# The opening of a hybrid decoder block: normalised on tokens and turned once, raw first products scaled in their banks

## The chip, the cores and the metric

The kernel runs on one core of a Trainium2 chip. A core has a matrix engine (TensorE, PE in the profile, with its weight loads as PEld), a vector engine (VectorE, DVE), a scalar engine (ScalarE, ACT), GpSimd (POOL) and SyncE (SP), which here only issues DMA transfers. Each engine works through its own queue in order and waits there for semaphores that others raise. The metric is the device time of one execution in microseconds; lower is better. Times of single instructions come from one profiled execution.

## The reference

One decoder layer for 256 tokens of width 2048 in float32: a half-step SwiGLU feed-forward, a mixer, a second half-step feed-forward and a last norm. Only the beginning of the first feed-forward matters here:

```python
def rms_norm(x, gain):
    var = jnp.mean(xf * xf, axis=-1, keepdims=True)
    return (xf * lax.rsqrt(var + NORM_EPS) * gain).astype(x.dtype)

def swiglu_ffn(x, w_gate, w_up, w_down):
    return (jax.nn.silu(x @ w_gate) * (x @ w_up)) @ w_down

x = x + 0.5 * swiglu_ffn(rms_norm(x, ffn1_norm), w_gate, w_up, w_down)
```

The norm's factor, rsqrt(var + eps), is one number for each token, and the gain is one number for each of the 2048 columns. `w_gate` and `w_up` are 2048 x 5632. So a product of tokens that are not yet scaled can be put right afterwards, row by row, while sums of products taken with Strassen's scheme need tokens that are scaled already.

## The kernel before, in words

**Layout.** `xres` holds x with tokens on the 128 partitions, in two halves (t = 0, 1), loaded in four pieces of 512 columns (`load_x(c)`, 0.5 MB each). TensorE needs x turned: columns on partitions. A column unit u (0 to 3) is 512 columns of x, four blocks j of 128. A turned unit is kept as a rounded high part and a remainder, low part. A weight block (`raw_g` of the gate matrix, `raw_u` of the up matrix) is 512 x 512, 1 MB; `load` issues its DMA from SP and `parts_of` splits it: ACT rounds it to the high part (`hi`, a CAST), DVE subtracts to get the low part (`lo`, a TENSOR_TENSOR). A product of a block with both token halves is 24 matmuls (`multiply`): 16 with `hi` and 8 with `lo`.

**The first 512 hidden columns** (the opening) are computed in the usual way from eight blocks, in the order g0, u0, g1, u1, g2, u2, g3, u3 (letter for the matrix, number for the column unit), into four PSUM banks, `ps_g` and `ps_u` for each token half. After that the hidden columns are computed 1024 at a time by Strassen's scheme for the units 0 and 1 and usually for the units 2 and 3 (`seven`): products named a, c, e, d, with block differences on DVE (`raw_g<-raw_g,raw_g`). The first of these, product a, then c, then e, follow the opening on TensorE. They need tokens that are scaled by the norm's factor, and three sums of them (`seven_of`, tiles `xs`).

**How the opening before makes its tokens.** `norm.turn` transposes unit u of the raw x on TensorE (`pt_n`), ACT takes it times the gain as the high part (`xT_n`), DVE takes the remainder. All eight blocks are multiplied by these raw units, and the factor comes in at the end, with the Silu and the last multiply (`sg<-ps_g,r_n`, `sg<-ps_u,r_n`). For the products that follow, the units are made a second time: `norm.factor` works the factor out from the sums of squares (`norm.squares`), `norm.rows` spreads it over the partitions (`diag_n`, `pb_n`, `bc_n`), `plain` puts high and low together again (units 0 and 1 on DVE, units 2 and 3 by ACT straight from the transpose's bank), and `normalise` multiplies by the spread factor on DVE (`v<-v,bc_n`), rounds on ACT (CAST `x<-v`) and subtracts on DVE (`x<-v,x`).

**What sets the order.** `Engine.pinned` (line 35) is a switch: while it is on, the instructions of PE, ACT and DVE stay in the order in which the program writes them; while it is off, a scheduler orders them. It is on until block u1 has been multiplied (line 532) and off from there. A loaded block takes one of three buffers (`raws`) and its load waits until DVE has made the low part of the block three before; SP issues loads in order, so a waiting load holds back those behind it. The first two blocks of `seven` go to two other buffers (`kept`). Splits have three buffers in rotation in all.

## Time and profile before

| | us |
|---|---|
| median of 3 runs (lowest to highest) | 1749.13 (1748.94 to 1749.91) |
| the profiled execution: its time | 1750.54 |
| the profiled execution: its span, first to last instruction | 1748.6 |
| TensorE busy | 1724.4 |
| VectorE busy | 1491.9 |
| ScalarE busy | 1045.3 |

The profiled execution is 1.41 us above the median of the runs; 1.94 us of its time lie around the span. A row of the timeline gives the start, the time from the first start to the last end of a merged group, the engine, the line (L42 is the wrapper through which PE, ACT and DVE instructions are recorded, so tiles tell more than lines), the operation, out<-in, and in brackets what ended idle time before it.

### The profile page before, as it was taken

How to read it: one execution, taken by the hardware profiler on the slowest of the kernel's cores; microseconds unless marked ns; L12 is line 12 of the kernel's file. 1: busy time of each engine (PE TensorE's matmuls, PEld its weight loads, DVE VectorE, ACT ScalarE, POOL GpSimd, SP SyncE). 2: the span in 40 equal slices, each digit the busy share in tenths (PEclk: the TensorE clock that was granted, in tenths of full speed). 3: DMA queues.
4: the chain of work that ended last, by engine and by line, in shares of the span. 5: the costliest groups of instructions: out<-in, count | busy, mean ns of one | idle time of the engine just before them, and what ended most of it. 6: DMA issues, size and time to landing. Idle time of an engine off the chain costs nothing. (4 is left out here: it accounts for less than half of the span.)

```text
span 1748.6 us, 20335 instructions
## 1 busy us (share of the span) xinstructions
PE 1724.4 (99%) x8031; PEld 1436.9 (82%) x8031; DVE 1491.9 (85%) x1247; ACT 1045.3 (60%) x1354; POOL 6.9 (0%) x32
## 2 busy tenths in 40 slices
PE   8899999999999999999999999999999999999997
PEld 6688788888888888888888888888788888888876
DVE  7988989889789888587987668989799887899885
ACT  6665565666465666574755455666566664656654
POOL 1000000000000000000000000000000000000000
PEclk9999999999999999999999999999999999999999
DMA  7465655674565665556555664574475546555743
GB/s 280 148 205 187 217 192 194 216 258 155 185 203 189 211 219 180 184 166 197 180 195 184 233 198 139 195 263 167 170 245 200 209 144 237 192 193 193 256 169 105
DMA packets 173904, 343.24 MB, mean 196 GB/s; under 512 B 5620, under 2 KB 8048, under 8 KB 173680
## 3 DMA queue, kind: packets, MB, share of 16 engines
q1 hardware_dynamic: 173344, 340.82, 56.9%
q8 instruction: 63, 1.03, 0.2%
q10 hardware_dynamic: 144, 1.05, 0.2%
q14 instruction: 33, 0.27, 0.0%
q0 software_dynamic: 320, 0.07, 0.0%
HBM read 339.82 MB, written 2.10 MB: 196 GB/s over the span
## 5 line engine op out<-in xcount | busy, mean ns | idle before, releaser
L42 ACT CAST hi_g_p<-raw_g 128x1024 fp32r<-128x1024 f32 x140 | 142.5, 1048 | 103.8 <-DVE raw_g L42 29.8
L42 DVE TENSOR_TENSOR lo_g_p<-raw_g,hi_g_p 128x2048 fp32r<-128x2048 f32 x70 | 159.6, 2288 | 31.9 <-ACT hi_g_p L42 31.8
L42 ACT CAST hi_u_p<-raw_u 128x1024 fp32r<-128x1024 f32 x140 | 140.8, 1048 | 74.0 <-PE ps_u_a L42 26.6
L42 DVE TENSOR_TENSOR lo_u_p<-raw_u,hi_u_p 128x2048 fp32r<-128x2048 f32 x70 | 159.1, 2286 | 19.5 <-ACT hi_u_p L42 19.2
L42 PE MATMUL ps_d<-hi_d,h 128*128 128x512 f32 x704 | 167.9, 390 | 0.0
L42 PEld LDWEIGHTS ps_d<-hi_d,h 128*128 128x128 f32 x704 | 131.5, 188 | 26.8
L42 PE MATMUL ps_in<-xT_nm,hi_in 128*128 128x512 f32 x640 | 153.3, 391 | 0.0
L42 PEld LDWEIGHTS ps_in<-xT_nm,hi_in 128*128 128x128 f32 x640 | 117.4, 188 | 23.2 <-ACT tha L42 0.4
L42 ACT CAST hi_d<-raw_d 128x1024 fp32r<-128x1024 f32 x88 | 88.2, 1047 | 68.0 <-PE ps_u_d L42 22.4
L42 DVE TENSOR_TENSOR lo_d<-raw_d,hi_d 128x2048 fp32r<-128x2048 f32 x44 | 100.6, 2290 | 31.4 <-ACT hi_d L42 31.4
L42 DVE TENSOR_TENSOR lo_in<-raw_in,hi_in 128x2048 fp32r<-128x2048 f32 x40 | 91.4, 2286 | 39.1 <-ACT hi_in L42 36.9
L42 ACT CAST hi_in<-raw_in 128x1024 fp32r<-128x1024 f32 x80 | 80.1, 1046 | 67.2 <-PE ps_in L42 45.7
L42 ACT CAST hi_d_p<-raw_d 128x1024 fp32r<-128x1024 f32 x84 | 84.3, 1046 | 50.8 <-DVE raw_d L42 39.6
L42 ACT CAST hi_g_x<-raw_g 128x1024 fp32r<-128x1024 f32 x80 | 81.5, 1048 | 45.5 <-PE ps_g_c L42 26.8
L42 DVE TENSOR_TENSOR lo_d_p<-raw_d,hi_d_p 128x2048 fp32r<-128x2048 f32 x42 | 95.4, 2288 | 11.7 <-ACT hi_d_p L42 11.6
L42 ACT CAST hi_u_x<-raw_u 128x1024 fp32r<-128x1024 f32 x80 | 80.5, 1047 | 33.3 <-PE ps_u_c L42 20.7
L42 DVE TENSOR_TENSOR raw_u<-raw_u,raw_u 128x2048 f32<-128x2048 f32 x40 | 91.6, 2290 | 8.7 <-DMA raw_u<-in_ffn_w_up_dram 8.0
L42 DVE TENSOR_TENSOR raw_g<-raw_g,raw_g 128x2048 f32<-128x2048 f32 x40 | 91.5, 2289 | 7.7 <-DMA raw_g<-in_ffn_w_gate_dram 7.3
L42 DVE TENSOR_TENSOR lo_g_x<-raw_g,hi_g_x 128x2048 fp32r<-128x2048 f32 x40 | 91.5, 2288 | 4.0 <-ACT hi_g_x L42 3.9
L42 DVE TENSOR_TENSOR lo_u_x<-raw_u,hi_u_x 128x2048 fp32r<-128x2048 f32 x40 | 91.4, 2285 | 0.8 <-ACT hi_u_x L42 0.6
L42 PE MATMUL ps_d<-lo_d,h 128*128 128x512 f32 x352 | 87.3, 389 | 0.0
L42 PEld LDWEIGHTS ps_in<-xT_nm,lo_in 128*128 128x128 f32 x640 | 82.1, 191 | 3.1
(346 smaller groups left out, 3583.6 us busy)
## 6 DMA issues: line engine op xcount, KB each, us to landing
raw_u<-in_ffn_w_up_dram SPq DMA_DIRECT2D x88, 1024.0 KB, 5.1
raw_d<-in_ffn_w_down_dram SPq DMA_DIRECT2D x88, 1024.0 KB, 5.1
raw_g<-in_ffn_w_gate_dram SPq DMA_DIRECT2D x87, 1024.0 KB, 5.1
raw_in<-in_w_in_dram SPq DMA_DIRECT2D x40, 1024.0 KB, 5.0
raw_o<-in_w_out_dram SPq DMA_DIRECT2D x16, 1024.0 KB, 5.1
xres<-in_x_dram SPq DMA_DIRECT2D x4, 512.0 KB, 8.5
fin<-in_final_norm_dram ACTq DMA_DIRECT2D x1, 1024.0 KB, 6.8
out_dram<-xres SPq DMA_DIRECT2D x4, 256.0 KB, 2.7
```

Source lines behind the costliest of these rows:

```text
L42: ins = getattr(self.engine, name)(*args, **kwargs)
```

## The change

The opening is written out as a function of its own, `begin`, in a fixed order from its first instruction to its last.

- Only unit 0 is still turned raw. Its two blocks, g0 and u0, are multiplied with the raw unit, and then their four banks are multiplied in place by the factor (`scaled`, a DVE TENSOR_SCALAR from PSUM to PSUM). The remaining blocks accumulate on top.
- The other units, and unit 0 a second time, are scaled on tokens by ACT (`tokens`: a copy of 128 x 512 with the factor as its scale), then transposed (`turned_tokens`), and split with the gain straight into the tiles `x` that the later products use (`high` on ACT, `low` on DVE). `rows` and `normalise` are no longer used in the opening; `plain` is used for the units 0 and 1 alone.
- x is loaded ahead: the pieces 1 and 2 right behind block g0, whose last piece now goes ahead of x; block u0 comes in two halves with piece 3 of x between them.
- Squares are shared between DVE and ACT (five and three; six and two before), and the factor is worked out before the second half of u0 is split.
- The first block of `seven` is loaded and split inside `begin` and handed over (`ready`). The Silu and the last multiply of the opening take no factor any more.

The second feed-forward keeps its way (`begin_after`). The diff, cut to its core:

```diff
+            def begin():
+                Engine.pinned = True
...
+                raw = {("g", 0): first_columns("g", 0, pieces=pieces)}
+                load_x(1)
+                load_x(2)
+                raw["u", 0] = first_columns(
+                    "u", 0, pieces=((0, 2), (2, 4)), loaded=lambda i: load_x(3) if i == 0 else None
+                )
+                for m, u in (("g", 1), ("u", 1)):
+                    raw[m, u] = first_columns(m, u)
...
+                norm.squares(0, (dve, dve))
+                for c in (1, 2):
+                    norm.squares(c, (dve, act))
+
+                def tokens(u):
+                    n = [keep(f"n{tag}_{u}_{t}") for t in range(NT)]
+                    for t in range(NT):
+                        act.activation(n[t], xres[:, t, u * CW : (u + 1) * CW], AF.Copy, scale=norm.r[:, t : t + 1])
+                    return n
+
+                def turned_tokens(u, n):
+                    pts = []
+                    for j in range(UK):
+                        pt = bank(f"pt{tag}_{u}_{j}")[:, :S]
+                        for t in range(NT):
+                            pe.transpose(pt[:, t * P : (t + 1) * P], n[t][:, j * P : (j + 1) * P], ident)
+                        pts.append(pt)
+                    return pts
+
+                def high(u, pts):
+                    for j, pt in enumerate(pts):
+                        act.activation(units[u][:, j, :S], pt, AF.Copy, scale=gain[:, UK * u + j : UK * u + j + 1])
+
+                def low(u, pts):
...
+                        dve.scalar_tensor_tensor(lo, pt, g, f32(hi), op0=ALU.mult, op1=ALU.subtract)
...
+                def scaled(banks):
+                    for t in range(NT):
+                        dve.tensor_scalar(banks[t], banks[t], norm.r[:, t : t + 1], None, op0=ALU.mult)
+
+                def work_out(i):
+                    if i == 2:
+                        norm.squares(3, (dve, act))
+                        norm.factor()
...
+                blk = parts("u", 0, between=work_out)
+                multiply(targets(ups, 0, norm.xT[0]), blk, js=(0, 1))
+                n, pts = tokens(1), []
+                multiply(
+                    targets(ups, 0, norm.xT[0]), blk, js=(2, 3), middle=lambda: pts.extend(turned_tokens(1, n))
+                )
+                scaled(gps)
...
+                def between_parts(i):
+                    if i == 2:
+                        high(1, pts)
+                        low(1, pts)
+
+                blk = parts("g", 1, between=between_parts)
+                raw["g", 2] = first_columns("g", 2)
+                n0 = tokens(0)
+                scaled(ups)
+                multiply(targets(gps, 1, units[1]), blk, True)
+                pts0 = turned_tokens(0, n0)
+                blk = parts("u", 1)
+                raw["u", 2] = first_columns("u", 2)
+                high(0, pts0)
+                low(0, pts0)
+                n2, pts2 = tokens(2), []
+                multiply(targets(ups, 1, units[1]), blk, True, middle=lambda: pts2.extend(turned_tokens(2, n2)))
+                plain(1, units[1])
+                plain(0, units[0])
+                blk = parts("g", 2)
+                raw["g", 3] = first_columns("g", 3)
+                high(2, pts2)
+                low(2, pts2)
+                n3, pts3 = tokens(3), []
+                multiply(targets(gps, 2, units[2]), blk, True)
+                sums()
+                blk = parts("u", 2)
+                raw["u", 3] = first_columns("u", 3)
+                sums()
+                multiply(targets(ups, 2, units[2]), blk, True, middle=lambda: pts3.extend(turned_tokens(3, n3)))
+                blk = parts("g", 3)
+                high(3, pts3)
+                low(3, pts3)
+                multiply(targets(gps, 3, units[3]), blk, True)
+                blk = parts("u", 3)
+                w11 = load(wg[: UK * P, CW : 2 * CW], f"g{tag}_first", kept=True)
+                ready.append((w11, parts_of(w11, f"g{tag}_first", split=lambda i: None)))
+                multiply(targets(ups, 3, units[3]), blk, True)
+                Engine.pinned = False
+                for t in range(NT):
+                    sg = keep(f"sg{tag}_0_{t}")
+                    act.activation(sg, gps[t], AF.Silu)
+                    dve.tensor_tensor(sg, ups[t], sg, op=ALU.mult)
...
-                follow = {
-                    (1, "g"): [norm.rows, lambda: plain(0)],
-                    (1, "u"): [flush, lambda: normalise(0), lambda: plain(1)],
-                    (2, "g"): [lambda: normalise(1), sums],
-                    (2, "u"): [lambda: normalise(2), sums],
-                    (3, "g"): [lambda: normalise(3)],
-                }
```

In three places the rows of the engines' queues show what moves. The names are tiles, with numbers that tell buffers apart.

On SP, from its second row, before: x and the blocks of unit 0.

```order
L93 DMA xres<-in_x_dram 128x2x512
L165 DMA raw_g_0_0_119<-in_ffn_w_gate_dram 128x512 x2
L93 DMA xres<-in_x_dram 128x2x512
L165 DMA raw_g_0_0_119<-in_ffn_w_gate_dram 128x2x512
L165 DMA raw_u_0_0_177<-in_ffn_w_up_dram 128x4x512
```

The same place after the change.

```order
L93 DMA xres<-in_x_dram 128x2x512
L165 DMA raw_g_0_0_119<-in_ffn_w_gate_dram 128x512 x2
L165 DMA raw_g_0_0_119<-in_ffn_w_gate_dram 128x2x512
L93 DMA xres<-in_x_dram 128x2x512 x2
L165 DMA raw_u_0_0_125<-in_ffn_w_up_dram 128x2x512
```

The rest of g0 goes ahead of x, pieces 1 and 2 of x go ahead of u0, and u0 comes in halves; piece 3 of x and the second half follow.

On DVE, before, from the low parts of the turned unit 2 to the low parts of block g2: the units 0 and 1 are being scaled (`v<-v,bc_n`), put together (`v<-xT_n`) and split again (`x<-v,x`).

```order
L42 SCALAR_TENSOR_TENSOR xT_n_2_319<-pt_n_11_338,cols_first,xT_n_2_319 128x256
L42 TENSOR_TENSOR v_0_0_302<-v_0_0_302,bc_n_300 128x512
L42 TENSOR_TENSOR v_0_1_303<-v_0_1_303,bc_n_300 128x512
L42 TENSOR_TENSOR v_1_0_376<-xT_n_1_194 128x512
L42 TENSOR_TENSOR x_0_369<-v_0_0_302,x_0_369 128x4x128
L42 TENSOR_TENSOR x_0_369<-v_0_1_303,x_0_369 128x4x128
L42 TENSOR_TENSOR v_1_1_377<-xT_n_1_194 128x512
L42 TENSOR_TENSOR lo_g_0_2_383<-raw_g_0_2_380,hi_g_0_2_382 128x1024 x2
```

On DVE, after, from the second scaled bank pair to the low parts of block g2.

```order
L42 TENSOR_SCALAR ps_u_0_1_118<-ps_u_0_1_118,r_n_216 128x512
L42 TENSOR_TENSOR lo_u_0_1_326<-raw_u_0_1_131,hi_u_0_1_325 128x1024 x2
L42 SCALAR_TENSOR_TENSOR x_0_198<-pt_0_0_313,cols_first,x_0_198 128x256
L42 SCALAR_TENSOR_TENSOR x_0_198<-pt_0_1_316,cols_first,x_0_198 128x256
L42 SCALAR_TENSOR_TENSOR x_0_198<-pt_0_2_319,cols_first,x_0_198 128x256
L42 SCALAR_TENSOR_TENSOR x_0_198<-pt_0_3_322,cols_first,x_0_198 128x256
L42 TENSOR_TENSOR v_1_0_381<-x_1_199 128x512
L42 TENSOR_TENSOR v_1_1_382<-x_1_199 128x512
L42 TENSOR_TENSOR v_0_0_385<-x_0_198 128x512
L42 TENSOR_TENSOR v_0_1_386<-x_0_198 128x512
L42 TENSOR_TENSOR lo_g_0_2_390<-raw_g_0_2_281,hi_g_0_2_389 128x1024 x2
```

The multiplications by the spread factor and the second split of each unit are gone; the low part of a unit is taken once, from the bank of the scaled transpose, and the banks are scaled in place.

On ACT, before, the high parts of block g3 stand ahead of the roundings of unit 1 and of the sums `xs`.

```order
L42 ACTIVATE v_3_1_389<-pt_n_15_412,cols_first 128x128
L42 CAST hi_g_0_3_506<-raw_g_0_3_504 128x1024 x2
L42 CAST x_1_443<-v_1_0_376 128x4x128
L42 CAST x_1_443<-v_1_1_377 128x4x128
L42 CAST hi_u_0_3_545<-raw_u_0_3_543 128x1024 x2
L42 CAST xs_0_450<-spare_452 128x4x128
```

On ACT, after, around the blocks u2 and g3.

```order
L42 CAST xs_0_433<-spare_435 128x4x128
L42 CAST hi_u_0_2_439<-raw_u_0_2_331 128x1024 x2
L42 CAST xs_0_433<-v_0_0_385 128x4x128
L42 CAST xs_1_434<-v_0_1_386 128x4x128
L42 CAST xs_1_434<-v_1_0_381 128x4x128
L42 CAST hi_g_0_3_492<-raw_g_0_3_395 128x1024 x2
L42 ACTIVATE x_3_201<-pt_3_0_472,cols_first 128x256
```

The roundings of the sums `xs`, whose inputs DVE makes, now stand ahead of the high parts of block g3, and these ahead of the high parts of unit 3.

More of the change, by code (lines that the diff above doesn't have):

```diff
@@ L212, in __init__, with squares @@
             self.ss = work.tile([P, NT, NC_D], F32, tag="ss", name=f"ss_{name}")
-        def squares(self, c, engine=None):
-            for t in range(NT):
+        def squares(self, c, engines=(act, act)):
+            for t, engine in enumerate(engines):
                 x, part = xres[:, t, c * CW : (c + 1) * CW], self.ss[:, t, c : c + 1]
@@ L345, in quad, with seven @@
         return tile.rearrange("p (j c) -> p j c", j=UK)
-    def seven(w, rows, cols, sf, xs, name, keep, done, between=None):
+    def seven(w, rows, cols, sf, xs, name, keep, done, between=None, ready=None):
         a, c, e, d = (bank(f"ps_{name}_{n}") for n in "aced")
@@ new lines, in begin_after @@
+                units.append(big(f"x{tag}_3"))
+                for t in range(NT):
+                    sg = keep(f"sg{tag}_0_{t}")
+                    act.activation(sg, ps["g", t], AF.Silu, scale=norm.r[:, t : t + 1])
+                    dve.scalar_tensor_tensor(
+                        sg, ps["u", t], norm.r[:, t : t + 1], sg, op0=ALU.mult, op1=ALU.mult
+                    )
+                    waiting.append((0, t, sg, False))
+            (begin if opening else begin_after)()
+            xs = list(enumerate(units))[2:]
```

107 lines of the change are left out of this document (47 added, 60 removed).

## The prediction

> **What bounds the kernel now.** First the page's busy times, then stages of the span (columns: stage, its length, busy time of PE, PEld, DVE, ACT and POOL, granted clock, DMA share, GB/s):
>
> ```profile
> PE 1724.4 (99%) x8031; PEld 1436.9 (82%) x8031; DVE 1491.9 (85%) x1247; ACT 1045.3 (60%) x1354; POOL 6.9 (0%) x32
> ...
> 13.00:29.00 16.00, 14.97 (x71) 12.14 (x72) 11.80 (x29) 12.07 (x18) 0.00 (x0) 1.00 1.05 387
> 29.00:76.00 47.00, 40.73 (x176) 32.13 (x175) 46.54 (x56) 31.36 (x56) 0.00 (x0) 0.93 0.40 135
> 76.00:140.00 64.00, 64.00 (x288) 53.07 (x288) 58.63 (x35) 42.05 (x48) 0.00 (x0) 1.00 0.66 227
> ```
>
> Over the whole span TensorE is the bound. The change touches only the first 76 us, and there it is another engine: from 29 to 76 us DVE is busy for 46.5 of 47 us, while TensorE idles and its clock falls. From 76 us TensorE is busy without a gap, so what the opening saves there reaches the end. TensorE's waits in the first 100 us, and its timeline, show the price:
>
> ```profile
> PE ps_g_c L42 <- ACT hi_g_p L42: 3.5, 1, 3.5
> PE ps_g_a L42 <- DVE lo_g_p L42: 1.6, 1, 1.6
> PE ps_u L42 <- DVE lo_u L42: 1.2, 2, 0.7
> PE ps_g L42 <- ACT hi_g L42: 0.8, 1, 0.8
> ...
> 11.63 0.39 PE L42 MATMUL ps_g<-lo_g,xT_n 128*128 128x512 f32 x1
> 13.21 0.50 PE L42 MATMUL ps_g<-lo_g,xT_n 128*128 128x512 f32 x1 [0.53 <-DVE lo_g L42]
> 15.58 1.03 PE L42 MATMUL pt_n<-ident,xres 128*128 128x128 f32 x8
> 16.37 3.90 PE L42 MATMUL ps_u<-hi_u,xT_n 128*128 128x512 f32 x16
> 28.54 0.60 PE L42 MATMUL pb_n<-diag_n,ones 128*128 128x128 f32 x4
> 28.98 1.12 PE L42 MATMUL pt_n<-ident,xres 128*128 128x128 f32 x8
> 68.20 3.78 PE L42 MATMUL ps_g_c<-hi_g_p,xs 128*128 128x512 f32 x8 [3.45 <-ACT hi_g_p L42]
> 72.87 1.98 PE L42 MATMUL ps_g_e<-hi_g_x,x 128*128 128x512 f32 x8
> 74.68 1.98 PE L42 MATMUL ps_g_c<-hi_g_x,x 128*128 128x512 f32 x8
> ```
>
> Eight matmuls take 1.81 us (72.87 to 74.68), so 0.227 each; eight transposes 0.79 (15.58 to 16.37). Between block g0's end (15.58) and product e (72.87) lie 57.3 us. The work in them is 192 matmuls (seven blocks of 24, products a and c of 12), 43.5 us, 24 transposes, 2.4, and the spread factor, 0.44: 46.3. So 11.0 us are lost to waits and to a slow clock. The start of product e is my measuring point.
>
> **The change, priced.** Durations of single steps on DVE and ACT:
>
> ```profile
> 14.47 2.36 DVE L42 TENSOR_TENSOR lo_u<-raw_u,hi_u 128x1024 fp32r<-128x1024 f32 x2
> 16.75 1.66 DVE L42 SCALAR_TENSOR_TENSOR xT_n<-pt_n,cols_first,xT_n 128x256 fp32r<-128x256 f32 x4
> 36.37 1.29 DVE L42 TENSOR_TENSOR x<-v,x 128x512 fp32r<-128x512 f32 x2
> 42.01 1.29 DVE L42 TENSOR_TENSOR v<-v,bc_n 128x512 f32<-128x512 f32 x2
> 63.41 1.41 DVE L42 SCALAR_TENSOR_TENSOR sg<-ps_u,r_n,sg 128x512 f32<-128x512 f32 x2
> L42 DVE SCALAR_TENSOR_TENSOR junkv_n<-xres 128x512 f32<-128x512 f32 x6 | 4.1, 689 | 0.1
> L42 DVE TENSOR_SCALAR diag_n<-ident,r_n 128x128 f32<-128x128 f32 x2 | 0.5, 280 | 0.0
> L42 DVE COPY bc_n<-pb_n 128x256 f32<-128x256 f32 x1 | 0.4, 424 | 3.5 <-PE pb_n L42 3.5
> ...
> 10.85 1.05 ACT L42 CAST hi_g<-raw_g 128x1024 fp32r<-128x1024 f32 x1 [1.71 <-DMA raw_g<-in_ffn_w_gate_dram]
> 13.39 2.00 ACT L42 CAST hi_u<-raw_u 128x1024 fp32r<-128x1024 f32 x2 [1.49 <-DMA raw_u<-in_ffn_w_up_dram]
> 16.00 1.57 ACT L42 ACTIVATE xT_n<-pt_n,cols_first 128x256 fp32r<-128x256 f32 x4 [0.61 <-PE pt_n L42]
> 17.45 0.65 ACT L42 ACTIVATE junk_n<-xres 128x512 f32<-128x512 f32 x1
> 18.21 0.63 ACT L42 ACTIVATE junk_n<-xres 128x512 f32<-128x512 f32 x1
> 42.73 1.23 ACT L42 CAST x<-v 128x512 fp32r<-128x512 f32 x2 [0.85 <-DVE v L42]
> 57.94 1.28 ACT L42 ACT_TABLE_LOAD   x1
> 59.23 0.69 ACT L42 ACTIVATE sg<-ps_g,r_n 128x512 f32<-128x512 f32 x1
> ```
>
> *DVE's work.* Removed: eight multiplications by the spread factor and eight second remainders at 0.645 (10.3 us), one square (0.7), the two diagonals and the copy that spread the factor (0.9). Added: four remainders of 256 at 0.41, since unit 0 is turned twice (1.65), and four scalings of a bank. No row shows such a scaling. The nearest is the last multiply, which reads a bank of 512 and takes 0.70; the copy of 256 from a bank took 0.42, so 512 need not take less. A scaling that reads and writes one bank might take twice 0.70. I take 0.72, keep 0.42 and 1.4 as ends: 2.9 us. Net, DVE has 7.4 us less to do. Its 3.5 us wait for `pb_n` goes too; but the fixed order brings waits of its own.
>
> *ACT's work.* Gone are the copies that put units 2 and 3 together (16 of 128 x 128) and eight roundings `x<-v` of 0.62. Added are eight token copies, priced between that rounding and the Silu with its factor (0.69), four high parts of 0.40 and a square. It has less to do in all, and only its order matters.
>
> *TensorE's work.* Eight transposes more (0.8), the spread less (0.44).
>
> *Loads.* The last piece of g0 landed at 10.85 behind 2 MB; now behind 1.5 MB. Half a MB at 387 GB/s takes 1.36 us, so it lands at 9.5. ACT and DVE need 2.2 us for its parts, TensorE reaches them at about 11.9 and no longer waits: g0 ends at 14.6 instead of 15.58. Block u0 landed at 13.39 behind 3 MB; piece 3 of x now comes behind 3.5 MB, at 14.7, the second half of u0 at 16.1. Behind these SP's queue now holds the first block of product a ahead of g2, and g2 waits until DVE has split u0 (19.3, below):
>
> ```profile
> raw_g<-in_ffn_w_gate_dram SPq DMA_DIRECT2D x87, 1024.0 KB, 5.1
> SPq L165 <- DVE lo_g_x L42: 22.8, 4, 12.6
> ```
>
> With 5.1 us to landing, and 2.7 more if the block ahead is still under way, g2 is there by 27.1; ACT wants it at 30.8. Later loads wait for DVE as before, which runs ahead of its old times. POOL's loads stay as they are. The four banks that a unit's transposes take at once are freed by DVE in time (unit 0's at 30.2, wanted for unit 2 at 32.0). All that costs nothing.
>
> *The new queue, laid out by these durations*, each engine in its order. TensorE waits five times:
> 1. u0, second half. x lands at 14.7; ACT squares half of it (0.76) and loads a table (1.28): 16.75. DVE, busy since 11.7 with five squares (0.73 apart) and the first half of u0 (1.18), has the mean at 16.85. After the root ACT rounds the second half, ready 18.1. TensorE was through at 17.3: 0.8 lost.
> 2. g1. DVE makes the second half of u0 (19.3), scales two banks (20.7), splits half of g1 (21.9), then the first low part of unit 1 (22.3). TensorE needs it at 21.85: 0.5.
> 3. g2. DVE: rest of unit 1 and g1 (24.7), two banks (26.1), u1 (28.5), unit 0 (30.2), four `plain` (32.7), g2 (35.0), first low part of unit 2 (35.5). TensorE: 34.85, so 0.7.
> 4. g3. DVE and ACT hand the sums `xs` to and fro: first sum 37.3, ACT rounds it (38.0), rounds u2 (39.9), DVE splits u2 (41.4), makes two sums (42.6), ACT rounds, DVE takes remainders (44.6) and the last sum (45.3), ACT rounds that (45.9) and only then g3 (47.8) and unit 3, first part at 48.3. TensorE was through with u2 at 47.0: 1.35.
> 5. g3 again. DVE's part of g3 ends at 49.3, the first low part of unit 3 is there at 49.8: 1.3 more.
>
> From there TensorE has 71 matmuls without a wait, 16.1 us: product e starts at 65.9. The low part of product c is ready at 64.4 and needed at 65.0, the tightest place. Laid out in the same way, the rows of before reach product e at 73.3 for the true 72.87.
>
> **The sum.** Earlier end of g0 1.0; lost time 11.0 less 4.6, 6.4; more transposes -0.4: 7.0 us. The profiled execution took 1750.54, so 1743.5 by it; off the median, 1749.13 - 7.0 = 1742.1.
>
> *A rule against it.* The table load above starts at 57.94 and the Silu follows at 59.23, so the switch took 1.28 us and nothing more. The Trainium skill (ScalarE: Activation LUTs, What ACT_TABLE_LOAD costs) adds a drain of 1.38 us to every switch. By that, step 1 would lose 2.1 us instead of 0.8 and the estimate would be 1743.4; this trace shows no such drain.
>
> **Rivals.**
>
> *The clock falls in the waits for g3 (chance 0.08).* Stages of five us around the long wait:
>
> ```profile
> 60.00:65.00 5.00, 2.60 (x9) 1.35 (x8) 5.00 (x6) 1.24 (x3) 0.00 (x0) 1.00 0.82 280
> 65.00:70.00 5.00, 1.80 (x4) 1.49 (x5) 4.97 (x3) 3.27 (x5) 0.00 (x0) 0.53 0.02 7
> 70.00:75.00 5.00, 5.00 (x19) 3.85 (x18) 5.00 (x3) 3.58 (x5) 0.00 (x0) 0.79 0.02 3
> ```
>
> After 3.45 us without work the twelve matmuls of product c took 4.67 us (68.20 to 72.87) instead of 2.72. Waits 4 and 5 make 2.6 us with one matmul between. If they cost the clock as well, 1.95 us go: 1744.1. Against it, waits of 1.6 and less left the clock at 1.00. The Trainium skill (TensorE: Matmul & The Clock Gate, Part 1: The HAM clock gate) says that the clock halves after an idle window of about 3.4 us, and that the window runs freely; by that, 2.6 us should not do it, and the 0.53 behind 3.45 us agrees.
>
> *Scaling a bank takes 1.4 us (0.07).* DVE is the chain in steps 2 to 5, so all four count: product e at 68.6, 1744.8. For it: reads and writes meet in one bank. Against it: the last multiply streams a bank at 0.70.
>
> *The gain is used up later (0.08).* Behind product e DVE is barely ahead of TensorE:
>
> ```profile
> 78.06 2.29 DVE L42 TENSOR_TENSOR lo_g_p<-raw_g,hi_g_p 128x2048 fp32r<-128x2048 f32 x1
> 81.02 1.07 PE L42 MATMUL ps_g_a<-lo_g_p,xs 128*128 128x512 f32 x4
> ```
>
> The low part used at 81.02 is ready at 80.35. If DVE or the loads didn't move up with TensorE, the waits would only move: 1749. Against it: SP's longest waits above are for DVE, which also runs 7 us earlier, and between 65 and 75 us the DMA engines are all but idle (0.02).
>
> *Slower: scaling a bank is slower still (0.07).* Each 0.1 us more for a scaling costs 0.4 at product e. At 2.4 us a scaling all is given back, at 3.3 the kernel is 3.6 us slower, 1753. Nothing shows a write from DVE into a bank, so I can't exclude it; DVE's reads of banks speak against it.
>
> **How the numbers follow.** My forecast has 0.70, at 1742.1. Its own range is 1740 to 1744: down to 1739.5 if steps 4 and 5 vanish, since they rest on single handovers. Clock and dear scaling, both still faster, reach 1744.8; with half of the no-change case the range is 1740 to 1746.5. Faster by over 0.2% (3.5 us, about what a measurement of this kernel can tell from no change) are forecast, clock and dear scaling, 0.85; within it 0.08; slower 0.07.
>
> **What would show it.** Product e starts near 66 us. TensorE's waits in the first 100 us are five of 0.5 to 1.4 us, the largest at g3 behind ACT and DVE, and none at products a and c. A TENSOR_SCALAR of 512 on DVE takes 0.7. The clock stays at 1.00 behind the first 15 us. From 76 us on TensorE has no gap. The forecast is wrong if scalings take over 1.4 us, if piece 3 of x lands after 17 us (each us late is a us lost), or if product c waits for its low part.

## The result, and the profile after

The changed kernel took 1742.09 us (median of five, 1741.62 to 1742.56) beside 1749.29 for the kernel before (1748.94 to 1750.37): a ratio of 0.9957, 95% interval 0.9943 to 0.9972. The forecast was 1742.1. The kernel was measured once more beside the last experiments and took 1744.02 there (1741.81 to 1744.53; ratio 0.9968, 0.9955 to 0.998). All ten times lie between 1741.6 and 1744.6, their median is 1742.4. Why they spread is taken up below and stays open.

The page's busy times of the changed kernel, and two stretches of its span (columns as in the prediction):

```profile
PE 1721.5 (99%) x8035; PEld 1436.3 (83%) x8035; DVE 1485.8 (85%) x1235; ACT 1043.5 (60%) x1344; POOL 6.9 (0%) x32
...
29.00:70.00 41.00, 39.18 (x179) 31.73 (x178) 38.17 (x42) 29.48 (x41) 0.00 (x0) 1.00 0.50 173
70.00:134.00 64.00, 64.00 (x289) 53.08 (x288) 57.88 (x34) 40.08 (x47) 0.00 (x0) 1.00 0.65 220
```

DVE has 6.1 us less to do in all, where 7.4 were forecast. Between 29 and 70 us TensorE is now busy for 39.2 of 41 us at a clock of 1.00; before, it was 40.7 of 47 at 0.93. From 70 to 134 us it has no gap, as before from 76 to 140.

TensorE's timeline (start, length, work, idle time ahead and what ended it). The waits are read from the weight loads, PEld, since a weight load in these rows starts no later than its first matmul:

```profile
14.48 1.98 PE L42 MATMUL ps_u<-hi_u,xT_n 128*128 128x512 f32 x8
17.70 1.69 PEld L42 LDWEIGHTS ps_u<-hi_u,xT_n 128*128 128x128 f32 x8 [0.76 <-ACT hi_u L42]
21.80 0.58 PEld L42 LDWEIGHTS ps_g<-hi_g,x 128*128 128x128 f32 x3 [0.39 <-DVE x L42]
35.01 3.28 PEld L42 LDWEIGHTS ps_g<-hi_g,x 128*128 128x128 f32 x15 [0.52 <-DVE x L42]
47.61 0.19 PEld L42 LDWEIGHTS ps_g<-hi_g,x 128*128 128x128 f32 x1 [1.17 <-ACT x L42]
49.08 3.28 PEld L42 LDWEIGHTS ps_g<-hi_g,x 128*128 128x128 f32 x15 [1.29 <-DVE x L42]
49.09 3.70 PE L42 MATMUL ps_g<-hi_g,x 128*128 128x512 f32 x15 [0.97 <-DVE x L42]
65.32 1.98 PE L42 MATMUL ps_g_e<-hi_g_x,x 128*128 128x512 f32 x8
```

Block u0 starts at 14.48, and product e at 65.32 instead of 72.87: 7.55 us earlier. The five waits are the five that were forecast. The last three lines are the place to remember: two waits at g3 with one matmul between, and behind them fifteen matmuls in 3.70 us, that is at full clock.

The steps that the prediction had to bound, on ACT and DVE (the lower two rows are groups: busy time, mean ns of one, idle time ahead):

```profile
15.06 1.28 ACT L42 ACT_TABLE_LOAD   x1
16.51 0.20 ACT L42 ACTIVATE s_n<-v_n 128x2 f32<-128x2 f32 x1 [0.17 <-DVE v_n L42]
...
L42 DVE TENSOR_SCALAR ps_g<-ps_g,r_n 128x512 f32<-128x512 f32 x2 | 1.4, 752 | 0.0
L42 ACT ACTIVATE n<-xres,r_n 128x512 f32<-128x512 f32 x8 | 5.4, 739 | 0.0
```

A bank's scaling takes 0.75 us. The table load ends at 16.34, and the root behind it then waits for DVE's mean alone.

### The profile page after: what moved, and what is told of

It is laid out like the page before. It is cut to its first block, busy times and chain, and to the rows that moved or that the text cites. A ratio compares the mean times of both kernels' runs of the same rounds, so it can differ in the third digit from the quotient of the medians.

```text
span 1740.3 us, 20333 instructions
## 1 busy us (share of the span) xinstructions
PE 1721.5 (99%) x8035; PEld 1436.3 (83%) x8035; DVE 1485.8 (85%) x1235; ACT 1043.5 (60%) x1344; POOL 6.9 (0%) x32
## 5 line engine op out<-in xcount | busy, mean ns | idle before, releaser
L42 ACT CAST hi_g_p<-raw_g 128x1024 fp32r<-128x1024 f32 x132 | 134.3, 1048 | 100.1 <-DVE raw_g L42 26.9
L42 DVE TENSOR_TENSOR lo_g_p<-raw_g,hi_g_p 128x2048 fp32r<-128x2048 f32 x66 | 150.4, 2288 | 31.6 <-ACT hi_g_p L42 31.4
L42 ACT CAST hi_d_p<-raw_d 128x1024 fp32r<-128x1024 f32 x84 | 84.3, 1046 | 51.0 <-DVE raw_d L42 39.2
L42 DVE TENSOR_TENSOR raw_g<-raw_g,raw_g 128x2048 f32<-128x2048 f32 x37 | 84.6, 2289 | 8.3 <-DMA raw_g<-in_ffn_w_gate_dram 7.9
```

The source lines that it names most:

```text
L42: ins = getattr(self.engine, name)(*args, **kwargs)
```

## The experiments

Product e is where the opening ends, so its start shows an effect more sharply than the whole time. The stretch behind it took from 1673.3 us (no scalings) to 1676.8 us (handovers filled) in the profiles of the changed kernel and its variants, at a mean clock of 0.999 in both. Product e is read from one profile of each kernel; the changed kernel's two agree within 0.04 us. Each kernel was measured beside the kernel before on the same chip.

| kernel | product e, us | median, us | ratio to before, 95% interval |
|---|---|---|---|
| before | 72.87 | 1749.2 to 1750.4 | |
| changed | 65.32 | 1742.09 | 0.9957, 0.9943 to 0.9972 |
| changed, again | 65.28 | 1744.02 | 0.9968, 0.9955 to 0.998 |
| before, less work on DVE | 69.63 | 1746.99 | 0.9981, 0.9972 to 0.999 |
| before, order fixed | 80.80 | 1757.39 | 1.0042, 1.0029 to 1.0055 |
| before, new loads | 76.37 | 1752.09 | 1.0017, 1.0008 to 1.0026 |
| changed, old loads | 67.83 | 1745.24 | 0.9976, 0.9967 to 0.9986 |
| changed, free order | 71.08 | 1748.01 | 0.9991, 0.9983 to 1.0 |
| changed, free behind unit 0 | 64.64 | 1741.08 | 0.9954, 0.994 to 0.9967 |
| changed, scalings twice | 68.58 | 1744.82 | 0.9969, 0.9958 to 0.998 |
| changed, no scalings | 65.56 | 1742.12 | 0.9962, 0.995 to 0.9975 |
| changed, longer wait at g3 | 68.82 | 1745.13 | 0.9972, 0.996 to 0.9983 |
| changed, g3 ahead of the sums | (order differs) | 1740.62 | 0.9953, 0.994 to 0.9965 |
| changed, handovers filled | 62.67 | 1739.01 | 0.9935, 0.9921 to 0.9948 |

### Which part of the change carries the gain: work, order or loads

**Less work on DVE, in the kernel before.**

```diff
 def normalise(u):
+    n = 1 if opening else UK
-    dve.tensor_tensor(v, v, norm.bc[:, hi]...to_broadcast([P, UK, P]), op=ALU.mult)
+    dve.tensor_tensor(v[:, :n], v[:, :n], norm.bc[:, hi]...to_broadcast([P, n, P]), op=ALU.mult)
```

> The kernel before, in which each of the eight multiplications by the spread factor covers a quarter of its columns (128x128 instead of 128x512), so that three quarters of the normalised plain units are left unscaled. An instruction goes from 0.645 to about 0.2 us: 3.6 us less on DVE; the scheduler keeps nearly the order of before, but takes product a behind u3. Theory A (DVE's work is the bound of the opening, a microsecond taken off it is a microsecond at product e, as the prediction took 7.4 us less work for about 7 us): product e 3.0 to 3.6 us earlier than 72.9, a part of the clock's loss behind the 3.45 us wait besides; the time 1744.5 to 1746. Theory B (it is handovers between ACT and DVE, not DVE's work): less than 1 us, 1748.3 and up.

DVE's group of these multiplications, and TensorE at products c and e:

```profile
L42 DVE TENSOR_TENSOR v<-v,bc_n 128x128 f32<-128x128 f32 x8 | 1.9, 280 | 0.0
...
65.17 3.68 PE L42 MATMUL ps_g_c<-hi_g_p,xs 128*128 128x512 f32 x8 [3.91 <-ACT hi_g_p L42]
...
69.63 2.00 PE L42 MATMUL ps_g_e<-hi_g_x,x 128*128 128x512 f32 x8
```

Product e came 3.24 us earlier, the time 3.4. But 0.5 us of that came ahead of all these multiplications: g0 ended at 15.06 instead of 15.58. That leaves 2.7 us. An instruction had become 0.28 us long, so 2.9 us had gone from DVE (8 x 0.365), and nearly all of it arrived at product e. The long wait at product c is still there (3.91) and still costs the clock: eight matmuls in 3.68. Theory A holds: in the kernel before DVE's work was the bound of the opening, not handovers. The scheduler also took product a behind u3, so the order is not quite that of before, and what that move did by itself is not shown.

**The order fixed, in the kernel before.**

```diff
-                    if (u, m) == (1, "u"):
-                        Engine.pinned = False
...
+            Engine.pinned = False
             if not opening:
                 units.append(big(f"x{tag}_3"))
```

> The kernel before, in which the whole opening keeps the written order on each engine (the flag stays up to the end of the loop over the blocks; behind it nothing else changes). Theory A (an order fixed by hand is worth nothing by itself, it is only as good as its sequence): in the written order each of the eight steps multiply, round, remainder on DVE waits for ACT's rounding, some 0.7 us each, on an engine that was busy for 46.5 of 47 us; product e starts 3 to 6 us later than the 72.9 of before and the time is 1752 to 1755. Theory B (the gain of the change is the fixed order): product e near 66, the time 1742 to 1744.

DVE in the middle of the opening, then TensorE:

```profile
44.86 0.69 DVE L42 TENSOR_TENSOR x<-v,x 128x512 fp32r<-128x512 f32 x1 [0.69 <-ACT x L42]
...
38.63 3.96 PE L42 MATMUL ps_g<-hi_g,xT_n 128*128 128x512 f32 x16 [2.40 <-ACT hi_g L42]
...
49.78 6.15 PE L42 MATMUL ps_u<-hi_u,xT_n 128*128 128x512 f32 x16 [5.37 <-ACT hi_u L42]
...
63.79 5.55 PE L42 MATMUL ps_g<-hi_g,xT_n 128*128 128x512 f32 x16 [2.21 <-ACT hi_g L42]
```

Product e came 7.9 us later, more than the 3 to 6 expected. The handover costs what was foreseen, 0.68 to 0.74 for seven of the eight steps (1.72 for the last). What I had left out is the clock: it fell at the wait of 5.37 us (sixteen matmuls in 6.15 instead of 3.95) and again behind one of 2.21 us (5.55). A fixed order is no gain by itself.

**The loads alone, in the kernel before.**

```diff
-                        raw = load(src, n, pieces, lambda i: load_x(1) if i == 1 else None)
+                        raw = load(src, n, pieces)
+                        load_x(1)
+                        load_x(2)
...
-                    raw = load(src, n)
-                    if opening and (u, m) == (0, "u"):
-                        load_x(2)
-                        load_x(3)
+                    if opening and (u, m) == (0, "u"):
+                        raw = load(src, n, ((0, 2), (2, 4)), lambda i: load_x(3) if i == 0 else None)
+                    else:
+                        raw = load(src, n)
```

> The kernel before with nothing changed but its loads, in the order of the changed kernel: g0 whole, x pieces 1 and 2, half of u0, x piece 3, the other half of u0. Theory A (the loads alone are worth nothing, since the later waits absorb the earlier end of g0; their 2.5 us in the changed kernel are the price that the fixed order would pay without them): g0's wait of 0.5 us goes and the one at g1 grows, u0's second half is rounded later; product e at 72.9 to 73.8, the time 1749.1 to 1750.0. Theory B (the earlier end of g0, 1.0 us in the prediction's sum, is a gain by itself): product e at 71.9, the time 1748.1.

ACT around the factor, then TensorE:

```profile
15.75 1.05 ACT L42 CAST hi_u<-raw_u 128x1024 fp32r<-128x1024 f32 x1 [1.66 <-DMA raw_u<-in_ffn_w_up_dram]
...
22.94 0.20 ACT L42 ACTIVATE s_n<-v_n 128x2 f32<-128x2 f32 x1 [2.00 <-DVE v_n L42]
...
24.13 5.57 PE L42 MATMUL ps_g<-hi_g,xT_n 128*128 128x512 f32 x16 [2.46 <-ACT hi_g L42]
...
66.48 2.07 PE L42 MATMUL ps_g_a<-lo_g_p,x 128*128 128x512 f32 x4 [1.61 <-DVE lo_g_p L42]
...
76.37 1.98 PE L42 MATMUL ps_g_e<-hi_g_x,x 128*128 128x512 f32 x8
```

The same place of product a in the kernel before:

```profile
63.55 1.20 PE L42 MATMUL ps_g_a<-lo_g_p,x 128*128 128x512 f32 x4 [1.60 <-DVE lo_g_p L42]
```

The loads alone make the old kernel slower, by 3.5 us at product e and 2.6 in the time. In its order ACT and DVE stop for u0's second half, which now lands last; the squares come behind it, the mean is late, and ACT, which waits 2.00 us for it, has g1 queued behind the root. TensorE's wait at g1 grows from 0.8 to 2.46 us, and behind it the clock falls (sixteen matmuls in 5.57 us, for 3.98). At product a it falls a second time, behind a wait of 1.61 us (four matmuls in 2.07 us, at 0.52), where the kernel before kept it behind 1.60 (1.20 us). So 1.2 of the 3.5 us are the later start of g1, 1.6 the clock there, and 0.6 the clock at product c. Theory A had the direction and up to 0.9 of it, not the clock. Theory B falls: the earlier end of g0 is no gain by itself.

**The old loads, in the changed kernel.**

```diff
-                raw = {("g", 0): first_columns("g", 0, pieces=pieces)}
-                load_x(1)
-                load_x(2)
-                raw["u", 0] = first_columns("u", 0, pieces=((0, 2), (2, 4)), loaded=...load_x(3)...)
+                raw = {("g", 0): first_columns("g", 0, pieces=pieces, loaded=lambda i: load_x(1) if i == 1 else None)}
+                raw["u", 0] = first_columns("u", 0)
+                load_x(2)
+                load_x(3)
```

> Only the order of the loads is that of before: g0 in its first two pieces, x piece 1, the rest of g0, block u0 whole, x pieces 2 and 3. All work and its order on the engines is that of the changed kernel. Theory (the fixed order needs x early, since ACT and DVE meet the squares of x ahead of u0's parts): the last piece of g0 lands at 10.9 instead of 9.1 and g0 waits 0.8 us again; the square of x piece 2 (14.7) holds ACT, u0's first half is rounded at 16.6 and TensorE waits 1.1 us there; x piece 3 (16.1) makes the factor late, 0.8 us at u0's second half. Product e starts at 67.5 us instead of 65.3, the time is 1742.1 + 2.2 = 1744.3. Rival (later waits for DVE absorb it, as an earlier start alone would be worth nothing in the kernel before): waits at g1, g2 and g3 shrink in return, product e at 65.3 to 66, the time 1742.1 to 1742.8.

TensorE's timeline:

```profile
13.37 0.50 PE L42 MATMUL ps_g<-lo_g_first,xT_n 128*128 128x512 f32 x1 [0.53 <-DVE lo_g_first L42]
...
16.68 2.11 PE L42 MATMUL ps_u<-hi_u,xT_n 128*128 128x512 f32 x8 [0.74 <-ACT hi_u L42]
...
20.18 2.12 PE L42 MATMUL ps_u<-hi_u,xT_n 128*128 128x512 f32 x8 [0.49 <-ACT hi_u L42]
...
67.83 1.98 PE L42 MATMUL ps_g_e<-hi_g_x,x 128*128 128x512 f32 x8
```

The waits come where they were foreseen, and u0's second half starts at 20.18 instead of 17.70. From there to product e it is 47.65 us, in the changed kernel 47.62 (17.70 to 65.32). So the 2.5 us are lost whole, ahead of u0's second half, and no later wait absorbs them. The same loads that cost the old order 3.5 us (2.2 of them by the clock) are worth 2.5 to the new one.

**The order free, in the changed kernel,** from the scaling of g0's banks on.

```diff
                 scaled(gps)
+                Engine.pinned = False
...
                 multiply(targets(ups, 3, units[3]), blk, True)
-                Engine.pinned = False
```

> All the work of the change and its loads, but behind the scaling of g0's banks the scheduler chooses the order on each engine. In the order that it chooses, ACT rounds g1 whole and half of u1 ahead of the table load and the root, and DVE splits half of g1 ahead of the mean of squares. Theory A (the fixed order is needed as much as the saved work): u1's first half lands near 21 us, so the root comes at 23.5 to 24 instead of 16.5 and the second half of u0 at 25; TensorE waits some 7 us there, longer than the 3.45 us behind which the clock fell in the kernel before, and the time goes back to 1748 to 1751. Theory B (the work taken off DVE carries the gain in whatever order): product e within 2 us of 65.3 and the time at 1742 to 1744.

ACT around the factor, then TensorE:

```profile
18.58 1.99 ACT L42 CAST hi_g<-raw_g 128x1024 fp32r<-128x1024 f32 x2 [3.29 <-DMA raw_g<-in_ffn_w_gate_dram]
21.36 1.04 ACT L42 CAST hi_u<-raw_u 128x1024 fp32r<-128x1024 f32 x1 [0.79 <-DMA raw_u<-in_ffn_w_up_dram]
22.42 1.28 ACT L42 ACT_TABLE_LOAD   x1
23.71 0.20 ACT L42 ACTIVATE s_n<-v_n 128x2 f32<-128x2 f32 x1
...
24.91 3.76 PE L42 MATMUL ps_u<-hi_u,xT_n 128*128 128x512 f32 x8 [7.11 <-ACT hi_u L42]
...
71.08 1.98 PE L42 MATMUL ps_g_e<-hi_g_x,x 128*128 128x512 f32 x8
```

Theory A holds: ACT's queue stands at loads of g1 and u1 that land at 18.6 and 21.4, the root stands behind them, TensorE waits 7.11 us, and almost all of the gain is lost (1748.01). But from u0's second half to product e it is only 46.2 us, although the fallen clock takes 1.8 of that. That is 3.2 us less than in the hand's order. But it doesn't show that the scheduler's order is better there: while TensorE waited, DVE had already split the whole of g1 and half of u1 (three steps of 1.14 us from start to start, 3.4 us), which in the hand's order come behind that point. The next run fixes the order up to there and so has no such head start.

**The order free behind unit 0's low parts.**

```diff
                 low(0, pts0)
+                Engine.pinned = False
                 n2, pts2 = tokens(2), []
...
                 multiply(targets(ups, 3, units[3]), blk, True)
-                Engine.pinned = False
```

> The changed kernel, its order fixed by hand up to the low parts of unit 0 and left to the scheduler behind them. The order that it chooses puts DVE's remainders of g3 between the differences of the sums and ACT's rounding of u2, g3 and u3 ahead of theirs. Theory (the fixed order earns its keep only around the factor, where the free order put roundings of g1 and u1 ahead of the root and lost 7.1 us; in the rest it costs the two waits at g3): no wait over 0.6 us from 18 us on, product e at 62.4 to 63.5, the time 1739.2 to 1740.3. Rival (the hand order is the better one all along): product e at 65.3 or later, 1742.1 or more.

TensorE's weight loads, then its matmuls:

```profile
48.41 3.28 PEld L42 LDWEIGHTS ps_g<-hi_g,x 128*128 128x128 f32 x15 [1.28 <-DVE x L42]
...
64.64 1.98 PE L42 MATMUL ps_g_e<-hi_g_x,x 128*128 128x512 f32 x8
```

It gains 0.7 us at product e, not the 2 to 3 expected, which fits a head start as the source of most of the 3.2 us: of the two waits at g3 one is left (1.28), behind sums that the scheduler put ahead of unit 3. So the hand's order is needed around the factor; behind it neither order is the best.

### What a bank's scaling costs

**Scaled twice, and not scaled.**

```diff
 def scaled(banks):
     for t in range(NT):
         dve.tensor_scalar(banks[t], banks[t], norm.r[:, t : t + 1], None, op0=ALU.mult)
+    for t in range(NT):
+        dve.tensor_scalar(banks[t], banks[t], 1.0, None, op0=ALU.mult)
```

> Each of the four banks is scaled a second time, by 1.0, so DVE gets four more instructions of 0.75 us, 2.8 to 3.0 us in all, between 20 and 29 us. Theory (DVE is the chain of the opening, TensorE only waits for it): laid out with the durations of the changed kernel's trace, the waits for the low part of unit 1 at g1 and of unit 2 at g2 grow to 1.8 and 1.7 us, the two waits at g3 stay, and product e starts at 67.8 us instead of 65.3; the time is 1742.1 + 2.5 = 1744.6. Rival (TensorE and ACT bound the opening, DVE's scalings lie beside their work): product e stays at 65.3 and the time at 1742.1. Second rival (a scaling that waits for a bank in use stops DVE for longer than its own length): more than 3.0 us, 1745.5 and up.

DVE, TensorE, and a stretch of two us behind the waits at g3:

```profile
18.75 1.41 DVE L42 TENSOR_SCALAR ps_g<-ps_g,r_n 128x512 f32<-128x512 f32 x2
20.07 1.29 DVE L42 TENSOR_SCALAR ps_g<-ps_g 128x512 f32<-128x512 f32 x2
...
50.73 5.30 PE L42 MATMUL ps_g<-hi_g,x 128*128 128x512 f32 x15 [0.98 <-DVE x L42]
...
68.58 1.98 PE L42 MATMUL ps_g_e<-hi_g_x,x 128*128 128x512 f32 x8
...
53.00:55.00 2.00, 2.00 (x6) 1.51 (x6) 2.00 (x2) 1.98 (x3) 0.00 (x0) 0.51 0.90 347
```

In the other kernel `scaled` is left empty:

```diff
 def scaled(banks):
-    for t in range(NT):
-        dve.tensor_scalar(banks[t], banks[t], norm.r[:, t : t + 1], None, op0=ALU.mult)
+    pass
```

> The changed kernel without the scaling of the four banks: the first unit's raw products stay unscaled, and DVE has four instructions of 0.70 us less between 18.8 and 25.3 us. Theory A (the prediction's line that each 0.1 us of a scaling costs 0.4 at product e): 2.8 us earlier, product e at 62.5, the time 1739.3. Theory B (DVE has slack at that place: it waits 0.58 us for ACT's part of unit 0 at 28.2, which hangs on TensorE's transposes behind g1, and 0.7 and more at each sum; a scaling of 0.7 us costs nothing and only a dearer one would): g1 starts up to 0.3 us earlier, all the rest stays, product e at 65.0 to 65.3, the time 1741.8 to 1742.1.

TensorE at u0's second half, DVE at unit 0, TensorE at product e:

```profile
17.94 2.11 PE L42 MATMUL ps_u<-hi_u,xT_n 128*128 128x512 f32 x8 [0.52 <-ACT hi_u L42]
...
28.46 1.66 DVE L42 SCALAR_TENSOR_TENSOR x<-pt,cols_first,x 128x256 fp32r<-128x256 f32 x4 [1.09 <-ACT x L42]
...
65.56 1.98 PE L42 MATMUL ps_g_e<-hi_g_x,x 128*128 128x512 f32 x8
```

Without the scalings nothing is gained at product e: 47.62 us from u0's second half, as with them. (The median, 1742.12, lies between the changed kernel's two, 1742.09 and 1744.02.) Where DVE was relieved it waited longer for ACT (1.09 instead of 0.58 us ahead of unit 0's low parts, and 0.9 at two other places). With them doubled product e came 3.26 us later, 0.8 more than expected, but only half of that is DVE's: g3's first matmul started 1.65 us later (49.26 us for 47.61), and 1.6 us more went because the clock fell behind the two waits at g3, which were as long as in the changed kernel. That the median, 1744.82, lies so near to the theory's 1744.6 is luck: DVE's part was smaller than its 2.5 us, and the clock, which it didn't have, made up for it. So the price isn't a straight line. The scalings as they are cost nothing; 2.6 us more of them cost 1.65.

### The clock at g3

**A longer wait.**

```diff
+                for i in range(3):
+                    idle = work.tile([P, CW], F32, tag="junk", name=f"idle_{i}", bufs=1)
+                    act.copy(idle, xres[:, 0, :CW])
                 blk = parts("g", 3)
```

> The changed kernel with three more copies of 128x512 by ACT (0.58 us each) ahead of its rounding of g3. By the layout TensorE then waits 2.5 to 2.9 us for g3 instead of 0.75, and 1.0 to 1.2 us once more for unit 3 after one matmul. Theory A (a wait under the 3.45 us behind which the clock fell in the kernel before leaves it alone): granted clock 1.00 behind the wait, eight matmuls in 1.8 us, product e at 67.0, the time 1743.8. Theory B (the prediction's rival: waits of 2.6 us already cost the clock): 0.5 to 0.8 behind it, product e at 68.5 to 69, the time 1745.5.

```profile
49.49 0.50 PE L42 MATMUL ps_g<-hi_g,x 128*128 128x512 f32 x1 [2.57 <-ACT x L42]
50.96 5.30 PE L42 MATMUL ps_g<-hi_g,x 128*128 128x512 f32 x15 [0.97 <-DVE x L42]
...
53.00:55.00 2.00, 2.00 (x7) 1.52 (x6) 2.00 (x3) 1.98 (x3) 0.00 (x0) 0.50 1.01 394
```

With 2.57 and 0.97 us of waiting the clock falls to 0.50, and fifteen matmuls take 5.30 us instead of 3.70. In this execution theory B holds, and the time (1745.13) lies nearest to its figure.

**The changed kernel again.** Nothing is edited.

> The changed kernel itself, beside the others. Product e at 65.3 and 1742.1 where TensorE's two waits at g3 (1.2 and 1.3 us with the weight loads, one matmul between) leave the clock at 1.00, as in its first profile. In the kernel with the scalings doubled the same two waits stood ahead of fifteen matmuls in 5.30 us instead of 3.70, so the clock fell there. Theory A (whether the two waits cost the clock depends on where they fall in the chip's own time, not on the kernel): some executions of this kernel pay 1.6 us too, its times spread from 1741.6 to 1744 and the median lies at 1742.1 to 1743.7. Theory B (1.3 us waits never cost the clock here): all times within 1741.6 to 1742.6.

```profile
49.04 3.71 PE L42 MATMUL ps_g<-hi_g,x 128*128 128x512 f32 x15 [0.97 <-DVE x L42]
...
65.28 1.98 PE L42 MATMUL ps_g_e<-hi_g_x,x 128*128 128x512 f32 x8
```

In the execution that was profiled (1741.81) the clock stayed, as in the first profile. The four others took 1743.09, 1744.02, 1744.37 and 1744.53, outside of the 1741.6 to 1742.6 of theory B. Their mean granted clocks were 0.998, 0.998, 0.997 and 0.997, that of the profiled one 0.999; half clock for 3.3 us would lower the mean by 0.001. So theory B falls. But theory A is not shown either. The median and the highest time lie above its 1743.7 and 1744. The mean clocks don't sort the executions: the five of the first measurement have 0.998 at 1741.62 to 1742.56, just as the ones of 1743.09 and 1744.02 here. And the two kernels below that have no wait at g3 spread as widely, 1739.87 to 1742.65 and 1738.53 to 1741.33. The doubled scalings show that the clock can fall behind these two waits; no trace of a slower execution of the changed kernel was taken, and the stretch behind product e, which differs by 3.5 us between profiles, could make its times without any fall at g3.

### What the waits at g3 are worth

**g3 ahead of the second half of the sums.**

```diff
                 raw["u", 3] = first_columns("u", 3)
-                sums()
                 multiply(targets(ups, 2, units[2]), blk, True, ...)
...
                 multiply(targets(gps, 3, units[3]), blk, True)
+                sums()
                 blk = parts("u", 3)
```

> One step is moved: the second half of the sums xs (three differences, three roundings, three remainders) comes behind g3 and unit 3's parts instead of ahead of them. No work is added or taken away. Theory (DVE's total of work up to product c's low part sets the end; the waits at g3 are only where its lateness shows): both waits at g3 (0.75 and 0.97 us) vanish and a wait of about 2.7 us comes up at the low part of product c, behind lo_g_p; product e starts at 65.6 instead of 65.3, the time is 1742.1 to 1742.7. Rival (the two waits at g3 are lost by the order alone and come off the end when g3 is served first): product e at 63.0 to 63.6, the time 1739.8 to 1740.4.

TensorE:

```profile
62.61 1.19 PE L42 MATMUL ps_g_e<-hi_g_x,x 128*128 128x512 f32 x4
...
65.03 1.18 PE L42 MATMUL ps_g_c<-lo_g_p,xs 128*128 128x512 f32 x4
...
66.88 2.11 PE L42 MATMUL ps_g_c<-hi_g_x,x 128*128 128x512 f32 x8 [0.35 <-ACT s_g L42]
```

Both waits at g3 are gone (the sixteen matmuls of its high part run through from 46.67 us). Product c's low part, used at 64.41 before, is now late, as the theory had it; but behind the part in fixed order the scheduler filled the hole with half of product e and with transposes. The next place that both kernels share is the first matmul of the down product, here and then in the changed kernel:

```profile
142.53 3.79 PE L42 MATMUL ps_d<-hi_d,h 128*128 128x512 f32 x16
```

```profile
143.27 3.79 PE L42 MATMUL ps_d<-hi_d,h 128*128 128x512 f32 x16
```

So 0.74 us are left as gain in these two profiles. The truth lies between the two theories: the waits moved, and a part was filled.

**The handovers filled.** Same work, other sequence on DVE and ACT:

```diff
+                dve.tensor_tensor(spare, a21, a22, op=ALU.add)
                 blk = parts("u", 2)
-                sums()
-                sums()
+                split_high(4, 0, spare)
+                dve.tensor_tensor(a21, a11, a21, op=ALU.subtract)
+                split_low(0, spare)
+                dve.tensor_tensor(a11, spare, a11, op=ALU.subtract)
+                dve.tensor_tensor(a12, a12, a11, op=ALU.subtract)
...
                 blk = parts("g", 3)
+                for i, n, q in rest: split_high(i, n, q)
                 high(3, pts3)
                 low(3, pts3)
+                for i, n, q in rest: split_low(n, q)
```

(The first `sums()` is a sum, its rounding and its remainder, the second three times a difference, its rounding and its remainder. `split_high` is ACT's rounding of a sum, `split_low` DVE's remainder. The low parts of unit 2 also come ahead of g2's.)

> The changed kernel with its steps in another order and nothing else: the three differences of the sums follow the first sum at once, instead of each waiting for ACT's rounding of the one before; ACT rounds u2 ahead of the first sum and g3 ahead of the three others; the remainders of the sums come behind unit 3's low parts; the low parts of unit 2 come ahead of g2's. Theory (DVE is the chain, and the 5 us that it idles between 36 and 52 us in handovers of the sums can be filled): laid out with the durations of the trace, the waits at g2 (0.5) and g3 (1.2 and 1.3 with the weight loads) vanish without a new one, product c's low part is ready 0.65 us ahead of its use; product e starts at 62.4 instead of 65.3, the time is 1742.1 - 2.9 = 1739.2. Rival (the waits move again, to product c, as they did in part when g3 was served first): product e at 64.6, the time 1741.4.

TensorE, and the stretch from u0's second half to product c:

```profile
62.67 1.98 PE L42 MATMUL ps_g_e<-hi_g_x,x 128*128 128x512 f32 x8
...
18.00:60.00 42.00, 42.00 (x201) 34.59 (x201) 40.68 (x52) 32.65 (x49) 0.00 (x0) 1.00 0.71 246
```

TensorE is busy for the whole of 42 us, and product e starts 2.65 us earlier than in the changed kernel (2.9 forecast). At 1739.01 (1739.2 forecast) it has the lowest median of the study. DVE is given no less work here, so the 2.65 us that the changed kernel still lost were lost in the handovers, not to DVE's total.

## Why the prediction was right, point by point

- **The sum.** 7.0 us were forecast at product e, 7.55 measured. From g0's end to product e it is 50.84 us (14.48 to 65.32), 46.7 of them work, so 4.1 us are lost for the 4.6 of the sum. That the first median, 1742.09, meets the forecast 1742.1 to 0.01 us is luck: product e gained 0.55 more than the sum, and the gain in the time was 7.2 us in the first measurement and 5.5 in the second.
- **The five waits** stand where they were put, and for the named reasons: 0.76, 0.39, 0.52, 1.17 and 1.29 us, for 0.8, 0.5, 0.7, 1.35 and 1.3.
- **DVE's work as the bound** of the kernel before: shown by the kernel with shorter multiplications (2.7 us at product e for 2.9 us of DVE's work), with product a moved as said there.
- **DVE as the chain in steps 2 to 5** of the changed kernel holds only in part. Four scalings less changed nothing at product e, and the same work in another order gained 2.65 us. What binds there is the handovers between TensorE, ACT and DVE: unit 0's parts hang on transposes that TensorE makes behind g1, and each sum waits for ACT's rounding.
- **DVE's saved work,** 7.4 us in the forecast, is 6.1 in the page's total. The total is no fine measure: with the scalings doubled it is 0.6 higher than in the changed kernel, for 2.6 us of added work.
- **The scaling** was taken at 0.72 and takes 0.75 (0.70 from start to start). But the line on it, that each 0.1 us of a scaling costs 0.4 at product e, is wrong: taking all four out gained nothing. I had laid the queue out at one price and drawn a straight line through it; without scalings DVE waits 0.9 us for ACT at g1 and again at u1, and 1.1 at unit 0, so the present price fills waits that would be there anyway. Above it the slope was 1.65 for 2.6, not 1 for 1. (By its own line a scaling of 3.3 would be 3.3 us slower, not 3.6.)
- **The term "earlier end of g0", 1.0.** The loads were worth 2.5 in the new order and cost 3.5 in the old one. As a term of its own it doesn't exist: in the eight profiles with the new loads and the fixed order around the factor, u0 starts between 14.22 and 14.91 us, and its second half between 17.62 and 17.94, whenever g0 ended. The sum came out since the lost time was laid out with these loads.
- **The rule on the table load** would have lost 2.1 us at the first wait. The wait was 0.76, and in the kernel with the free order the load runs from 22.42 to 23.70 and the root starts at 23.71. No drain is to be seen on either side.
- **The rival of the clock,** given 0.08, had a weak argument against it: waits up to 1.6 us had left the clock at 1.00 in one profile, and with new loads a wait of 1.61 us did not. With the scalings doubled the clock did fall behind these same two waits, for 1.6 us, so the rival is possible. Whether it occurs in the changed kernel is not shown: both of its profiles have 1.00 there. The second median, 1744.02, is close to its price of 1744.1, but the spread of the times has other sources as well.
- **The scaling beyond 1.4 us, the gain used up later, the slower case:** none occurred. TensorE has no gap from 70 to 134 us, and the first matmul of the down product starts at 143.27 instead of 150.82, still 7.55 us earlier.

So the mechanism was right for what the change removes: DVE's work bounded the kernel before, and taking it off moved product e. Loads and order were right only together. What is left in the changed kernel was put in the right places, but read too much as DVE's work and too little as handovers. The clock was left out of the sum, and what it takes from this kernel is open.

## What to carry to other kernels

Price an edit on a chain by laying the whole queue out twice, at both ends of its price: a slope read off one layout misleads where the engine has waits of its own. Loads, order and saved work can be worth nothing or less one by one; undo each alone before crediting it. Where two engines hand work to and fro, issue the next independent step between: here that was worth 2.65 us at product e with no instruction saved.

## What the runs showed of the hardware

The clock fell behind shorter waits than I had expected, and not each time. Two waits of 1.17 and 1.29 us with one matmul between left it at 1.00 in four profiles (the changed kernel twice, with old loads, and without scalings) and halved it in one (doubled scalings, 0.51). A wait of 2.46 us lowered it (the kernel before with new loads: sixteen matmuls in 5.57 us), one of 2.40 us did not (the kernel before in fixed order: sixteen in 3.96), and in that same kernel one of 2.21 us, 1.2 us behind one of 0.83, did (5.55). One of 1.61 us lowered it (new loads: four matmuls in 2.07 us), one of 1.60 us at the same place did not (the kernel before: 1.20). Each fall behind g3 cost 1.6 us. The Trainium skill (TensorE: Matmul & The Clock Gate, Part 1: The HAM clock gate) describes a window of about 3.4 us that runs freely, without regard to the kernel; the different outcome of equal waits agrees with that. That only gaps above 3.4 us matter, as its section on HAM oscillation puts it, does not agree with the 2.46. How much idle time in which stretch makes the clock fall is not shown by these runs.
